# Two blocks of adaLN scale and shift in a two-layer trunk: raw weights as the stationary side of single-column matmuls

## The chip, the cores and the metric

The kernel runs on one core of one Trainium2 chip. The metric is the device time of one execution in microseconds; lower is better. All inputs, weights and results are float32 in device memory, and the kernel is one launch.

## The reference, cut to what matters

Two layers, each with a token mixer and a SwiGLU feed-forward part, over 512 tokens of 1024 features. Ahead of each part the tokens are normalized and modulated by scale and shift, which come from a conditioning vector `c` through a 1024 x 3072 matrix:

```
def ada_modulation(c, w, b):
    m = jax.nn.silu(c) @ w + b
    shift, scale, gate = jnp.split(m, 3, axis=-1)
...
    shift, scale, gate = ada_modulation(c, mix_ada_w[i], mix_ada_b[i])
    h = rms_norm(x, mix_pre_g[i]) * (1.0 + scale) + shift
    y = stick_breaking_mixer(h, sb_w_qkv[j], sb_w_o[j])
```

The change touches only the very first modulation (`mix_ada_w[0]`), and of it only the scale and shift of features 0 to 255. The rest of the work (attention with stick-breaking weights, three more modulations, the gated mixer, two feed-forward parts) is the same in both kernels.

## The kernel before, in words

Features lie in 8 blocks of 128. At the start the kernel loads the four token tiles of `x` (128 x 1024 each), normalizes them (`norm0`), transposes them with TensorE into feature-major tiles `xhT` (`turn0`; tile `tp` in the profile), applies scale and shift to one feature block at a time (`h0`, line 702, on ScalarE), and splits the result into a rounded high part `hTh` and a remainder `hTl`. Every product of the model is then three matmuls: high by high, high by low, low by high. The weights are split in the same way into `wh` (ScalarE, line 161) and `wl` (VectorE, line 162).

With block 0 of `h` the kernel starts the value projection (tiles `v`, weights "wv") and the query and key projection of the first pair of heads (`pq` and `pk`, weights "wqk"). It accumulates over the 8 feature blocks in order, so each block's scale and shift, for which the raw modulation matrix must be multiplied by `silu(c)` (the column tile `sc`), stands ahead of its matmuls.

The sums of `silu(c)` by the raw matrix are made in two ways. Blocks 0 and 1 are loaded as two raw tiles each (`ada`, 128 x 4 x 256: four input blocks, 128 columns of scale and 128 of shift), and go through `row0` and `scales`: TensorE multiplies a single column of `sc` as weights by 256 moving columns and sums over the 8 input blocks into one row in PSUM; VectorE copies the row; two matmuls with one partition turn it into two columns; VectorE adds the bias and multiplies. Blocks 2 to 7 are loaded two at a time as four raw tiles (128 x 2 x 512) and summed over input blocks on VectorE, eight instructions for each pair of blocks (`ada0_sum`, tile `acc`); four matmuls with a moving column of ones (`sums0`) then sum over the partitions and give columns.

```
    def sums0(ps, acc, k):
        for i in range(4):
            mm(ps[:, i : i + 1], acc[:, i * P : (i + 1) * P], onec, False, i == 3)
```

A scheduler lays out each engine's instructions from the order of the code and its own costs; in the part of the program that the change touches nothing else holds them in the order in which they are written. On the chip each engine runs its own list strictly in that order and waits on semaphores. Loads are issued from SyncE's queue, also in order; two buffers hold raw weights ("raw"), so a load of the next weights waits until the split of those two before is done.

In the profile one f32 matmul is two records of PE (and two weight loads of PEld); a transpose or a matmul of split operands is one.

Of the kernel before, what the change touches and what calls it, by code (L numbers as in the profile page):

```python
# [8 lines left out]
F32 = mybir.dt.float32  # L9
# [4 lines left out]
P = 128  # L14
# [3 lines left out]
KD = D // P  # L18
# [13 lines left out]
def trunk(ctx: ExitStack, tc: tile.TileContext, A: dict, out: bass.AP):  # L32
# [17 lines left out]
    def nm(s):  # L50
        uid[0] += 1
        return f"{s}_{uid[0]}"
# [4 lines left out]
    def bank(name, tag="b"):  # L57
        return psum.tile([P, 512], F32, tag=tag, bufs=6 if tag == "b" else 2, name=nm(name))
# [19 lines left out]
    dve = Vector()  # L78

    def pe_op(b):  # L80

        if pe["chain"] and pe["prev"] is not None:
            order(b, pe["prev"])
        pe["prev"] = b

    def order(b, before):
        tc.add_manual_dep(
            b.ins, before.ins.name,
            mybir.DependencyInfo(mybir.DependencyClass.NoSync, mybir.DependencyReason.DATA),
            reason="order",  # L90
        )

    def mm(o, l, r, start, stop, after=None):
        b = nc.tensor.matmul(o, l, r, start=start, stop=stop, skip_group_check=True)  # L94
        pe_op(b)
        if after is not None:
            order(b, after)
# [29 lines left out]
    raws = []  # L127
# [107 lines left out]
    def wget(src, look=3):  # L235

        n = taken[0]
        taken[0] += 1
        while len(got) < min(n + 1 + look, len(stream)):
            wemit()  # L240
        assert stream[n][3] == src, (stream[n][3], src)
        return got[n]
# [44 lines left out]
    stp = st0.__enter__()  # L287

    def ada0_raw(b, q):

        nk, n = (4, 256) if b < 2 else (2, 512)
        raw = stp.tile([P, nk, n], F32, tag="ra", bufs=8, name=nm("ada0"))
        load(raw[:], A["ada0s"][b, q] if b < 2 else A["ada0p"][b - 2, q])
        return raw
# [3 lines left out]
    x0, a0 = [], []  # L298
# [12 lines left out]
    a1 = [ada0_raw(1, q) for q in range(2)]  # L311
# [5 lines left out]
    oneb = consts.tile([P, 2], F32, name="oneb")  # L317
# [3 lines left out]
    sc = consts.tile([P, KD], F32, name="sc")  # L321
# [271 lines left out]
    def norm0(tt):  # L593
        xt = x0[tt]
        junk = npool.tile([P, D], F32, tag="n", name=nm("junk"))
        sx = small.tile([P, 1], F32, tag="sx", name=nm("sx"))
        act.activation(junk[:], xt, AF.Square, accum_out=sx[:])
        sd, r1 = rms(sx[:])
        dve.reciprocal(r1[:], sd[:])
        dve.tensor_scalar(xt, xt, r1[:, 0:1], None, ALU.mult)  # L600

    def turn0(tt):
        xt = x0[tt]
        for q in range(2):
            ps = bank("tp0")
            for k in range(4):
                kk = q * 4 + k
                transpose(ps[:, k * P : (k + 1) * P], xt[:, kk * P : (kk + 1) * P])
            for k2 in range(2):
                dst = xhT[q * 2 + k2][:, :, tt * P : (tt + 1) * P]  # L610
                src = ps[:, k2 * 256 : (k2 + 1) * 256].rearrange("p (a b) -> p a b", a=2)
                if q and tt < 2:
                    dve.tensor_copy(dst, src)
                else:
                    act.activation(dst, src, AF.Copy)
# [47 lines left out]
    def cols0(k):  # L663

        ps = bank("ab0", "p")
        mm(ps[:, 0:4], ident, add[:, k : k + 2, :].rearrange("p n a -> p (n a)"), True, False)
        return ps
# [8 lines left out]
        )  # L676
        return ab

    def row0(raws):

        ps = bank("ab0", "p")
        for q, raw in enumerate(raws):
            for k in range(4):
                mm(ps[0:1, :256], sc[:, q * 4 + k : q * 4 + k + 1], raw[:, k, :], q + k == 0, q * 4 + k == 7)
        row = stp.tile([P, 256], F32, tag="row", bufs=2, name=nm("row"))
        dve.tensor_copy(row[0:1, :], ps[0:1, :256])
        ps = bank("ab0", "p")
        for i in range(2):
            mm(ps[:, i : i + 1], row[0:1, i * P : (i + 1) * P], oneb[0:1, 0:1], True, True)
        return ps  # L690

    def scales(ps, k):

        ab = small.tile([P, 2, 2], F32, tag="ab", name=nm("ab"))
        dve.tensor_tensor(ab[:, 0, :], ps[:, :2], add[:, k, :], ALU.add)
        dve.tensor_tensor(ab[:, 0, :], ab[:, 0, :], mul[:, k, :], ALU.mult)
        return ab

    def h0(ab, i, k):

        xk = xhT[k // 2][:, k % 2, :]
        act.activation(xk, xk, AF.Identity, scale=ab[:, i, 0:1], bias=ab[:, i, 1:2])
        h, l = hTk(hT, k, 0, T)
        split(h, l, xk)
# [9 lines left out]
    norm0(1)  # L714
    turn0(0)
    norm0(2)
    ab0 = row0(a0)
    turn0(1)
    norm0(3)
    turn0(2)  # L720
# [1 line left out]
    wv0.append(wget(("wv", 0, 0), 0))  # L722
    a2 = [ada0_raw(2, q) for q in range(4)]
    h0(scales(ab0, 0), 0, 0)
    ab1 = row0(a1)
    wqk0.append(wget(("wqk", 0, 0), 0))
    vb = [bank("v0") for _ in range(NT)]
    pq0, pk0 = bank("pq"), bank("pk")
# [5 lines left out]
    for b in range(1, 4):  # L734

        ps = cols0(2 * b)
# [818 lines left out]
```

## Time and profile before

| | |
|---|---|
| time, median of 3 runs | 1135.93 us (1134.57 to 1136.39) |
| the profiled execution's own time | 1133.95 us |
| its span, first to last instruction | 1132.2 us |
| PE busy | 1110.9 us, 98% of the span |
| PEld, DVE, ACT busy | 999.9, 933.0, 596.6 us |
| granted TensorE clock, mean | 0.998 |

Engines are PE (matmuls), PEld (weight loads, beside PE), DVE (VectorE), ACT (ScalarE), POOL and SP (load queue). "L94" is a line of the kernel, here the helper that records every matmul, so that matmuls are told apart by their tiles: "ab<-ada,sc" writes tile `ab` from `ada` and `sc`. A row's idle time names what the engine waited for. The profiled execution was 1.98 us under the median of the timed runs.

### The profile page before, as it was taken

The page shows a single profiled execution, that of the slowest core. Times are in us where ns is not written, and L with a number is a line of the kernel's source. Part 1 is how long each engine was busy: PE and PEld are TensorE (multiplying, and loading weights), DVE is VectorE, ACT ScalarE, POOL GpSimd, SP SyncE. Part 2 cuts the span into 40 slices and gives each one's busy share as a digit, 9 for nine tenths or more (in the row PEclk, how much of TensorE's full clock was granted, in tenths as well). Part 3 has the DMA queues.
Part 4 walks back from the last instruction along what each step waited for, and adds up shares of the span by engine and source line. Part 5 has one row for each costly group of instructions (what it writes and reads, how often), then busy time and mean ns, then how long its engine had stood idle before and what let it go on. Part 6 is the DMA issues. An engine that isn't in the chain of part 4 may idle for free.

```text
span 1132.2 us, 18659 instructions
## 1 busy us (share of the span) xinstructions
PE 1110.9 (98%) x7436; PEld 999.9 (88%) x7436; DVE 933.0 (82%) x1223; ACT 596.6 (53%) x985; POOL 29.5 (3%) x53
## 2 busy tenths in 40 slices
PE   6999999999999999999999999999999999999997
PEld 4787878788999999998888988988999999999996
DVE  4988999958989898778686865759979898789996
ACT  6445655656655555572153624537455555465752
POOL 0120100000000000010000100001000000000000
PEclk9999999999999999999999999999999999999999
DMA  8876434214344343348886483324243434223242
GB/s 322 336 238 213 147 98 134 93 59 158 122 150 131 128 151 117 129 136 310 269 275 218 150 280 110 131 94 160 83 132 115 164 130 146 70 85 99 90 154 106
DMA packets 51356, 176.39 MB, mean 156 GB/s; under 512 B 6074, under 2 KB 9146, under 8 KB 51268
## 3 DMA queue, kind: packets, MB, share of 16 engines
q1 hardware_dynamic: 48708, 166.81, 43.6%
q0 software_dynamic: 2560, 8.39, 2.0%
q8 instruction: 58, 0.95, 0.3%
q14 instruction: 30, 0.25, 0.1%
HBM read 164.69 MB, written 8.39 MB: 153 GB/s over the span
## 4 chain that ended last, share of the span: by engine, by line
PE 88%; DVE 5%; ACT 3%; DMA 2%; issue 1%; SPq 0%; DVEq 0%; ACTq 0%
PE r L94 32%; PE y L94 16%; PE v L94 8%; PE pqk L94 7%; PE X L94 4%; PE gu L94 4%; PE Y L94 3%; PE u L94 3%; PE av L94 2%; PE z L94 2%; PE tw L102 1%; PE Z L94 1%; PE W L94 1%; PE tp L102 1%; PE ab L94 1%
## 5 line engine op out<-in xcount | busy, mean ns | idle before, releaser
L94 PE MATMUL r<-Sh,wl 128*128 128x256 f32 x608 | 170.0, 280 | 0.0
L94 PE MATMUL r<-Sh,wh 128*128 128x256 f32 x608 | 169.9, 279 | 0.0
L94 PE MATMUL r<-Sl,wh 128*128 128x256 f32 x608 | 169.8, 279 | 0.0
L161 ACT ACTIVATE wh<-raw 128x1024 fp32r<-128x1024 f32 x87 | 91.6, 1059 | 113.3 <-PE y L94 57.5
L94 PE MATMUL y<-wh,as 128*128 128x512 f32 x480 | 150.7, 391 | 0.0
L117 ACT ACTIVATE wh<-f 128x1024 fp32r<-128x1024 f32 x87 | 92.3, 1061 | 91.3 <-PE r L94 66.4
L70 DVE TENSOR_TENSOR wl<-f,wh 128x1024 fp32r<-128x1024 f32 x87 | 106.4, 1222 | 38.9 <-ACT wh L117 38.8
L162 DVE TENSOR_TENSOR wl<-raw,wh 128x1024 fp32r<-128x1024 f32 x87 | 105.8, 1221 | 38.2 <-ACT wh L161 37.5
L94 PEld LDWEIGHTS r<-Sl,wh 128*128 128x128 f32 x608 | 114.2, 188 | 0.0
L94 PEld LDWEIGHTS r<-Sh,wl 128*128 128x128 f32 x608 | 114.2, 188 | 0.0
L94 PEld LDWEIGHTS r<-Sh,wh 128*128 128x128 f32 x608 | 114.1, 188 | 0.0
L94 PEld LDWEIGHTS y<-wh,as 128*128 128x128 f32 x480 | 90.1, 188 | 18.6
L94 PE MATMUL y<-wl,as 128*128 128x512 f32 x240 | 93.8, 391 | 0.0
L94 PE MATMUL r<-hTh,wh 128*128 128x256 f32 x304 | 88.9, 293 | 0.6 <-DVE gu L70 0.6
L94 PE MATMUL r<-hTl,wh 128*128 128x256 f32 x304 | 84.8, 279 | 0.0
L94 PE MATMUL r<-hTh,wl 128*128 128x256 f32 x304 | 80.0, 279 | 0.0
L94 PEld LDWEIGHTS r<-hTh,wh 128*128 128x128 f32 x304 | 57.0, 188 | 5.9 <-DVE gu L70 2.4
L94 PE MATMUL r<-hTh,b 128*128 128x256 f32 x304 | 59.8, 279 | 0.0
L117 ACT ACTIVATE wh<-rawx 128x1024 fp32r<-128x1024 f32 x38 | 40.3, 1061 | 33.4 <-PE r L94 30.8
L94 PEld LDWEIGHTS r<-hTl,wh 128*128 128x128 f32 x304 | 57.2, 188 | 0.1
L94 PEld LDWEIGHTS r<-hTh,wl 128*128 128x128 f32 x304 | 55.0, 188 | 0.0
L94 PE MATMUL gu<-hTh,wh 128*128 128x256 f32 x192 | 54.0, 281 | 0.0
(272 smaller groups left out, 2960.7 us busy)
## 6 DMA issues: line engine op xcount, KB each, us to landing
rawada<-in_ada SPq DMA_DIRECT2D x80, 512.0 KB, 4.9
rawy<-in_wy SPq DMA_DIRECT2D x38, 512.0 KB, 3.5
rawx<-in_wx SPq DMA_DIRECT2D x38, 512.0 KB, 4.1
raw<-in_wdown SPq DMA_DIRECT2D x22, 512.0 KB, 4.6
raw<-in_wdn SPq DMA_DIRECT2D x22, 512.0 KB, 3.5
raw<-in_wqk SPq DMA_DIRECT2D x16, 512.0 KB, 4.5
ada<-in_ada0p SPq DMA_DIRECT2D x12, 512.0 KB, 9.0
raw<-in_wgu SPq DMA_DIRECT2D x12, 512.0 KB, 3.5
```

What stands on the lines that cost most here:

```text
L70: b = getattr(nc.vector, op)(*args, **kw)
L94: b = nc.tensor.matmul(o, l, r, start=start, stop=stop, skip_group_check=True)
L102: last_tp[0] = nc.tensor.transpose(o, i, ident)
L117: act.activation(hi, src, AF.Copy)
L161: act.activation(h[:], raw[:], AF.Copy)
L162: last_low[0] = nc.vector.tensor_tensor(l[:], raw[:], h[:].bitcast(F32), ALU.subtract)
```

## The change

The row is gone. `raw0` makes the two columns directly: for each of the 8 input blocks and for scale and shift, the raw 128 x 128 tile is the weights and the column of `sc` is what moves. That is 16 f32 matmuls for a feature block, all accumulated in one PSUM bank, in place of 8 matmuls with 256 moving columns, one copy on VectorE and two single-partition matmuls. `scales` and everything behind it are as they were, and no load is added, removed or moved in its queue.

```diff
-    def row0(raws):
+    def raw0(raws):
         ps = bank("ab0", "p")
         for q, raw in enumerate(raws):
             for k in range(4):
-                mm(ps[0:1, :256], sc[:, q * 4 + k : q * 4 + k + 1], raw[:, k, :], q + k == 0, q * 4 + k == 7)
-        row = stp.tile([P, 256], F32, tag="row", bufs=2, name=nm("row"))
-        dve.tensor_copy(row[0:1, :], ps[0:1, :256])
-        ps = bank("ab0", "p")
-        for i in range(2):
-            mm(ps[:, i : i + 1], row[0:1, i * P : (i + 1) * P], oneb[0:1, 0:1], True, True)
+                kk = q * 4 + k
+                for i in range(2):
+                    mm(
+                        ps[:, i : i + 1], raw[:, k, i * P : (i + 1) * P], sc[:, kk : kk + 1],
+                        kk + i == 0, kk + i == KD,
+                    )
         return ps
...
-    ab0 = row0(a0)
+    ab0 = raw0(a0)
...
-    ab1 = row0(a1)
+    ab1 = raw0(a1)
```

The scheduler also lays the first instructions of three engines out differently. Behind this stage the lists of all engines are the same in both kernels but for a few matmuls and casts that change places with a neighbour.

On PE, from the second transposed token tile on, before (`ab_45` is block 0's bank, `ab_47` its columns, `ab_65` block 1's bank; `x_2`, `x_3` and `x_4` are token tiles):

```order
L102 MATMUL tp_49_207<-identt,x_2_95 128x128 x4
L94 MATMUL ab_45_186<-ada_5_101,sc 1x256 x4
L94 MATMUL ab_45_186<-ada_6_103,sc 1x256 x4
L102 MATMUL tp_54_222<-identt,x_3_97 128x128 x4
L102 MATMUL tp_55_229<-identt,x_3_97 128x128
L94 MATMUL ab_47_197<-oneb,row_195 128x1 x2
L102 MATMUL tp_55_229<-identt,x_3_97 128x128 x3
L102 MATMUL tp_56_236<-identt,x_4_99 128x128 x4
L102 MATMUL tp_57_243<-identt,x_4_99 128x128 x4
L94 MATMUL ab_65_268<-ada_8_107,sc 1x256 x4
L94 MATMUL ab_65_268<-ada_9_109,sc 1x256 x4
L94 MATMUL v_70_286<-wh_250,hTh_132 128x512
```

and in the changed kernel, at the same place (block 0's bank is `ab_45`, block 1's is `ab_63`; `ab_78` is the bank of blocks 2 and 3):

```order
L102 MATMUL tp_47_210<-identt,x_2_95 128x128 x4
L94 MATMUL ab_45_186<-sc,ada_5_101 128x1 x8
L102 MATMUL tp_52_225<-identt,x_3_97 128x128 x4
L102 MATMUL tp_53_232<-identt,x_3_97 128x128 x4
L94 MATMUL ab_45_186<-sc,ada_6_103 128x1 x8
L102 MATMUL tp_54_239<-identt,x_4_99 128x128 x4
L102 MATMUL tp_55_246<-identt,x_4_99 128x128 x4
L94 MATMUL ab_63_271<-sc,ada_8_107 128x1 x8
L94 MATMUL ab_78_334<-add,identt 128x4
L94 MATMUL v_66_292<-wh_253,hTh_132 128x512
L94 MATMUL ab_63_271<-sc,ada_9_109 128x1 x8
L94 MATMUL v_66_292<-wl_254,hTh_132 128x512
```

The second half of block 1's sums moved behind the first value matmul, which needs block 0's `hTh`.

On ACT, from the first weight cast to the second, before (`wh_250` is the first "wv" tile, `wh_282` the first "wqk" tile, `ab_262` holds block 0's columns; the scale of block 1 is the next row):

```order
L161 ACTIVATE wh_250<-raw_105 128x1024
L615 ACTIVATE xhT_128<-tp_54_222 128x2x128
L615 ACTIVATE xhT_129<-tp_54_222 128x2x128
L615 ACTIVATE xhT_130<-tp_55_229 128x2x128
L615 ACTIVATE xhT_131<-tp_55_229 128x2x128
L615 ACTIVATE xhT_128<-tp_56_236 128x2x128
L615 ACTIVATE xhT_129<-tp_56_236 128x2x128
L615 ACTIVATE xhT_130<-tp_57_243 128x2x128
L615 ACTIVATE xhT_131<-tp_57_243 128x2x128
L702 ACTIVATE xhT_128<-xhT_128,ab_262 128x512
L117 ACTIVATE hTh_132<-xhT_128 128x512
L161 ACTIVATE wh_282<-raw_111 128x1024
```

and in the changed kernel, from the last token tile's evacuation on (`wh_253` and `wh_288` are the same two weights, `ab_265` and `ab_310` the columns of blocks 0 and 1):

```order
L615 ACTIVATE xhT_128<-tp_54_239 128x2x128
L615 ACTIVATE xhT_129<-tp_54_239 128x2x128
L615 ACTIVATE xhT_130<-tp_55_246 128x2x128
L615 ACTIVATE xhT_131<-tp_55_246 128x2x128
L161 ACTIVATE wh_253<-raw_105 128x1024
L702 ACTIVATE xhT_128<-xhT_128,ab_265 128x512
L117 ACTIVATE hTh_132<-xhT_128 128x512
L702 ACTIVATE xhT_128<-xhT_128,ab_310 128x512
L161 ACTIVATE wh_288<-raw_111 128x1024
L117 ACTIVATE hTh_132<-xhT_128 128x512
```

Both casts of weights moved: the first from ahead of all eight evacuations to behind them, the second from ahead of block 1's scale to behind it.

On DVE, from block 0's `hTl` to the end of the first eight sums of `ada0_sum`, before:

```order
L70 TENSOR_TENSOR hTl_133<-xhT_128,hTh_132 128x512
L162 TENSOR_TENSOR wl_283<-raw_111,wh_282 128x1024
L70 COPY row_277<-ab_65_268 1x256
L70 SCALAR_TENSOR_TENSOR acc_318<-ada_60_254,sc,acc_318 128x512
L70 TENSOR_TENSOR ab_304<-ab_67_279,add 128x2
L70 SCALAR_TENSOR_TENSOR acc_318<-ada_60_254,sc,acc_318 128x512
L70 TENSOR_TENSOR ab_304<-ab_304,mul 128x2
L70 SCALAR_TENSOR_TENSOR acc_318<-ada_61_256,sc,acc_318 128x512 x2
L70 TENSOR_TENSOR hTl_133<-xhT_128,hTh_132 128x512
L70 SCALAR_TENSOR_TENSOR acc_318<-ada_62_258,sc,acc_318 128x512 x2
L70 SCALAR_TENSOR_TENSOR acc_318<-ada_63_260,sc,acc_318 128x512 x2
```

and in the changed kernel:

```order
L70 TENSOR_TENSOR hTl_133<-xhT_128,hTh_132 128x512
L70 TENSOR_TENSOR ab_310<-ab_63_271,add 128x2
L70 TENSOR_TENSOR ab_310<-ab_310,mul 128x2
L162 TENSOR_TENSOR wl_289<-raw_111,wh_288 128x1024
L70 TENSOR_TENSOR hTl_133<-xhT_128,hTh_132 128x512
L70 SCALAR_TENSOR_TENSOR acc_324<-ada_58_257,sc,acc_324 128x512 x2
L70 SCALAR_TENSOR_TENSOR acc_324<-ada_59_259,sc,acc_324 128x512 x2
L70 SCALAR_TENSOR_TENSOR acc_324<-ada_60_261,sc,acc_324 128x512 x2
L70 SCALAR_TENSOR_TENSOR acc_324<-ada_61_263,sc,acc_324 128x512 x2
```

Four of the eight sums stood ahead of block 1's `hTl`; now all eight stand behind it, and block 1's columns and the split of the "wqk" weights stand ahead of them.

## The prediction

> **What bounds the kernel now.** First the page: busy times and the chain of work that ended last.
>
> ```profile
> PE 1110.9 (98%) x7436; PEld 999.9 (88%) x7436; DVE 933.0 (82%) x1223; ACT 596.6 (53%) x985; POOL 29.5 (3%) x53
> PE 88%; DVE 5%; ACT 3%; DMA 2%; issue 1%; SPq 0%; DVEq 0%; ACTq 0%
> ```
>
> TensorE is the bound of the whole. What the start is worth is read from the busy time in windows:
>
> ```profile
> 35.00:40.00 5.00, 4.83 (x21) 4.02 (x22) 4.86 (x8) 1.70 (x3) 0.00 (x0) 1.00 1.00 393
> 40.00:45.00 5.00, 4.62 (x26) 3.60 (x24) 4.83 (x8) 2.16 (x4) 0.00 (x0) 1.00 1.03 417
> 45.00:50.00 5.00, 5.00 (x22) 4.16 (x23) 4.86 (x9) 1.35 (x2) 0.00 (x0) 1.00 1.03 416
> 50.00:60.00 10.00, 10.00 (x49) 8.38 (x49) 9.86 (x11) 4.51 (x8) 3.43 (x8) 1.00 0.61 203
> ```
>
> PE is full from 45 us on, so a microsecond by which the matmuls there come later is a microsecond at the end. VectorE is full too from 35 to 60 us (4.86, 4.83, 4.86, 9.86): it has no room to give a delay back. The stage itself is in the chain of waits, in order of time (start, length, what):
>
> ```profile
> 10.29 1.97 PE tp L102 x8
> 12.26 4.46 PE ab L94 x16
> 16.71 0.70 PE tp L102 x5
> 17.41 0.53 PE ab L94 x4
> 17.94 1.35 PE tp L102 x11
> 19.30 3.54 PE ab L94 x16
> 24.88 0.55 PE ab L94 x4
> 35.17 3.02 PE v L94 x12
> 38.19 0.68 PE pq L94 x3
> ```
>
> The two rows of sums (4.46 and 3.54) and the turns into columns (0.53, 0.55) lie on the chain: 9.08 us of PE. The timeline shows who stands beside them (start, length, engine):
>
> ```profile
> 13.85 0.13 PEld L94 LDWEIGHTS ab<-ada,sc 128*1 128x1 f32 x1 [0.30 <-issue]
> 14.09 1.06 ACT L161 ACTIVATE wh<-raw 128x1024 fp32r<-128x1024 f32 x1
> 14.18 2.03 PEld L94 LDWEIGHTS ab<-ada,sc 128*1 128x1 f32 x10 [0.20 <-issue]
> 18.46 1.77 ACT L615 ACTIVATE xhT<-tp 128x256 f32<-128x256 f32 x6 [0.46 <-PE tp L102]
> 20.05 0.85 ACT L702 ACTIVATE xhT<-xhT,ab 128x512 f32<-128x512 f32 x1
> 20.94 0.63 ACT L117 ACTIVATE hTh<-xhT 128x512 fp32r<-128x512 f32 x1
> 21.48 1.04 ACT L161 ACTIVATE wh<-raw 128x1024 fp32r<-128x1024 f32 x1
> 22.55 1.23 DVE L162 TENSOR_TENSOR wl<-raw,wh 128x1024 fp32r<-128x1024 f32 x1 [0.25 <-ACT wh L161]
> 24.02 0.73 DVE L70 SCALAR_TENSOR_TENSOR acc<-ada,sc,acc 128x512 f32<-128x512 f32 x1
> 25.45 0.16 DVE L70 TENSOR_TENSOR ab<-ab,add 128x2 f32<-128x2 f32 x1 [0.70 <-PE ab L94]
> 26.19 0.15 DVE L70 TENSOR_TENSOR ab<-ab,mul 128x2 f32<-128x2 f32 x1
> 27.89 0.69 DVE L70 TENSOR_TENSOR hTl<-xhT,hTh 128x512 fp32r<-128x512 f32 x1
> 28.50 3.11 DVE L70 SCALAR_TENSOR_TENSOR acc<-ada,sc,acc 128x512 f32<-128x512 f32 x4
> 31.89 0.95 PE L94 MATMUL ab<-oneb,acc 128*128 128x1 f32 x8
> 32.80 0.50 PE L94 MATMUL pk<-hTh,wl 128*128 128x512 f32 x1
> ```
>
> Two readings matter. VectorE's eight sums `acc` begin at 24.02, four of them ahead of block 1's `hTl` (27.89), and end at 28.50 + 3.11 = 31.61; TensorE reaches the matmuls that need them at 31.89. They meet within 0.3 us: whatever delays `acc` from here delays PE. And the first sums of a row run in a slower gear: their weight loads are 0.42 apart until 13.85, then ten in 2.03, which is why the same 16 records took 4.46 us the first time and 3.54 the second.
>
> **The change, part by part.** *New matmuls.* The case has their like: the single-column matmuls behind `acc`, 128 x 128 f32 weights and one moving column. Eight records from 31.89 to the next start at 32.80 are 0.91/8 = 0.114 us each. A block's 16 matmuls are 32 records, 3.65 us; both blocks 7.30, against 9.08 now: PE works 1.78 us less.
>
> *Up to block 0's `hTh`.* PE now does 32 of these records and 16 transposes (1.35/11 = 0.123 each) from 12.26: 3.65 + 1.97, to 17.9. The slow gear lasts until 14.1; bounds for the price of a record in it are 0.114 and twice that, which puts the end between 17.9 and 18.8. I take 18.1, against 19.30: 1.2 us earlier. ACT's last evacuation ends 18.46 + 1.77 = 20.23 now, 0.93 behind the last transpose, so at 19.0. But the 1.06 us cast of the first weights, which now fills an idle stretch at 14.09, stands behind the evacuations: 20.1. Then 0.85 + 0.63: `hTh` at 21.6, where it is now (20.94 + 0.63 = 21.57). The gain is gone; VectorE's row copies cost nothing that ends late.
>
> *Up to block 1's `hTh`.* The second half of block 1's sums, 16 records, 1.82 us, is queued on PE behind the first value matmul (3.02/12 = 0.25 with its wait, 0.68/3 = 0.227 in a stream), which waits for that `hTh`. So 21.7 + 0.23 + 1.82 = 23.75, VectorE's two small steps (0.16, 0.15) and semaphores: columns at 24.1. ACT scales (0.85) to 24.95, then must cast the "wqk" weights (1.04, to 26.0), then `hTh` at 26.65.
>
> *VectorE.* Its list is strict: split of "wqk" after 26.0 (1.23), to 27.3; block 1's `hTl` (0.69), to 28.0; only then eight sums. One is 3.11/4 = 0.78: 6.2, to 34.2, against 31.61. The raw tiles do not matter: `acc` runs from 24.02 today, so they are there.
>
> *PE then.* Behind 23.75 it has 11 + 12 value records and six of `pq`, 6.6 us, and 0.25 for bias columns: done at 30.6. It waits 3.6 us for `acc`, with `pk` and the next block's matmuls queued behind. The columns' matmuls start at 34.2 instead of 31.89: 2.3 us late. In the next block the sums start behind two weight splits, as now, from a VectorE that is 2.6 us late:
>
> ```profile
> 36.75 4.68 DVE L70 SCALAR_TENSOR_TENSOR acc<-ada,sc,acc 128x512 f32<-128x512 f32 x6
> 41.65 0.95 PE L94 MATMUL ab<-oneb,acc 128*128 128x1 f32 x8
> ```
>
> They end at 41.43 now and PE is there at 41.65, another meeting within 0.3; late by 2.6 and 2.3, they meet again. I carry 2.6 us to the end, between 1.9 (the gear's best case, and waits somewhat shorter) and 3.2 (the slow record price).
>
> *The clock.* A wait of 3.6 us is new. What such a wait does stands at the end of the trace, in the windows after the last matmul:
>
> ```profile
> 1124.60:1126.80 2.20, 0.21 (x1) 0.00 (x0) 1.16 (x2) 1.02 (x3) 0.00 (x0) 1.00 0.68 238
> 1126.80:1132.00 5.20, 0.00 (x0) 0.00 (x0) 1.71 (x4) 0.00 (x0) 0.00 (x0) 0.50 0.29 101
> ```
>
> About 2 us after PE's last matmul the granted clock is 0.50. At the start it took from 10.29 to 14.18, 3.9 us of work, to get from 0.42 to 0.22 a step (the clock column shows 1.00 there, the steps show the gear). If the clock falls in the new wait, some 3.9 us run at half speed: up to 1.9 us of work lost, less where PE waits anyway (the value matmuls at 35.17 follow a wait for `hTh`). I take 1.5, between 0 and 2.2.
>
> Sum: 2.6 + 1.5 = 4.1 us on the profiled execution's 1133.95, 1138.05. That execution was 1.98 us under the median of 1135.93; added, **1140.0 us**.
>
> **The rivals.** *No fall of the clock*: PE's wait is too short for it, or broken into pieces. Then 2.6 remains: 1138.5. For it: today's waits of a microsecond or so leave the gear alone.
>
> *Slow gear until the value matmuls*: single-column matmuls may not count as work for the clock. Against it, nothing in this trace shows them at the start; for it, the gear rose only during the row sums, not during 1.97 us of transposes. Then 16 transposes cost 0.12 more each (1.97/8 = 0.25 against 0.123), 2.0, and the 48 records on the path to block 1's columns 0 to 0.114 more each: 2.0 to 7.5 in all. By the middle, less the 0.2 that the 18.1 holds already, 4.5 on top of the forecast's 1140.0: 1144.5 (1142 to 1147.5).
> [...]
>
> *The other side: PE's shorter work decides.* 1.78 us less, on a chain that is nearly all PE: 1135.93 - 1.8 = 1134.1. It needs `acc` at 31.61 or sooner, so block 1's `hTl` done by 25.4 instead of 28.0: that is where it tips. The strict lists of ACT and VectorE, with the two casts moved, speak against it; it happens if the sums are not really behind `hTl`, or the casts are hidden.
>
> *Swallowed*: a later wait that depends on a fixed time takes the 2.6 us back; 1135.9. PE full from 45 us on speaks against it.
>
> **How the numbers follow.** Chances: forecast 0.47 (1140.0), no fall of the clock 0.18 (1138.5), slow gear 0.25 (1144.5), PE's shorter work 0.05, swallowed 0.05. About 0.2%, 2.3 us, is what a measurement here can tell from no change: from 1133.7 to 1138.2 is the same. Of the no-fall case 0.13 lies above that, 0.05 within. So slower 0.47 + 0.25 + 0.13 = 0.85; same 0.05 + 0.05 = 0.10, the swallowed case and the rest of no-fall; faster 0.05, the shorter work, counted whole though 1134.1 is just at the bound. The range, 1137.0 to 1145.5, takes the no-fall case down to 1.1 us and the slow gear to somewhat over its middle; the two unlikely cases and a third of the slow gear, under 0.2, are left out.
>
> **What would show it.** Right: about 64 records `ab<-sc,ada` at 0.11 to 0.12 us each once the gear is up; block 0's `hTh` near 21.6; the first `acc` only near 28 and the last one ending near 34; a PE wait of some 3.6 us for `acc` ahead of `ab<-oneb,acc`; matmul steps twice as long for a few microseconds behind it; PE full from about 48 us on. Wrong in size: steps of 0.42 at the first value matmuls (slow gear), or none behind the wait (no fall). Wrong in kind: `acc` ended before 32, or PE not waiting for it.

## The result: slower by 0.7%, and the profile after

| | before | after |
|---|---|---|
| time, median of the runs | 1135.91 us (1133.98 to 1136.85, 6 runs) | 1145.32 us (1140.75 to 1147.62, 6 runs) |
| ratio of the times, 95% interval | | 1.0073 (1.0052 to 1.0094) |
| the profiled execution's own time | 1133.95 us | 1145.34 us |
| its span | 1132.2 us | 1143.5 us |
| first rise of the granted clock in the trace | 14.07 us | 35.93 us |

The ratio is 8.3 us (5.9 to 10.7); the two medians lie 9.4 us apart. Two lines of the page after, busy time and the chain that ended last:

```profile
PE 1119.5 (98%) x7460; PEld 1013.3 (89%) x7460; DVE 933.2 (82%) x1221; ACT 596.9 (52%) x985; POOL 29.5 (3%) x53
PE 80%; DVE 8%; DMA 7%; ACT 3%; issue 2%; SPq 0%; DVEq 0%; ACTq 0%
```

PE is busy for 8.6 us more (1119.5 against 1110.9), though at the prices of the prediction it had 1.8 us less to do. The chain of waits of the changed kernel says where (start, length, what):

```profile
10.69 1.97 PE tp L102 x8
12.66 3.20 PE ab L94 x16
15.87 1.81 PE tp L102 x8
17.68 3.21 PE ab L94 x16
20.88 1.81 PE tp L102 x8
22.69 3.63 PE ab L94 x18
26.32 0.63 PE v L94
26.95 3.22 PE ab L94 x16
...
30.59 0.81 ACT xhT L702
31.40 0.96 ACT wh L161
...
33.52 0.69 DVE hTl L70
34.21 0.67 DVE acc L70
...
53.80 3.01 PE v L94 x12
```

Sixteen single-column records take 3.20 to 3.22 us on the chain, 0.200 each, and eight transposes 1.81, 0.226 each: both at the price of a slow clock from the first to the last. Behind them stand ACT's scale, the "wqk" cast, block 1's `hTl` and then the sums. The last row is the start of the twelve value matmuls of feature block 4; in the kernel before that group stands here:

```profile
44.93 3.02 PE v L94 x12
```

That is 8.87 us later in the changed kernel. I use this group as the marker in all runs below but e9, whose order differs there. The timeline of the changed kernel shows the change of gear and the meeting of `acc` with PE:

```profile
25.06 0.63 ACT L117 ACTIVATE hTh<-xhT 128x512 fp32r<-128x512 f32 x1
33.58 0.63 PE L94 MATMUL v<-wh,hTh 128*128 128x512 f32 x1
34.01 0.63 PE L94 MATMUL v<-wl,hTh 128*128 128x512 f32 x1
34.12 6.26 DVE L70 SCALAR_TENSOR_TENSOR acc<-ada,sc,acc 128x512 f32<-128x512 f32 x8
36.05 0.39 PE L94 MATMUL v<-wh,hTh 128*128 128x512 f32 x1
36.28 0.39 PE L94 MATMUL v<-wl,hTh 128*128 128x512 f32 x1
40.44 1.05 PE L94 MATMUL ab<-oneb,acc 128*128 128x1 f32 x8 [0.60 <-DVE acc L70]
```

The value matmuls are 0.43 apart at 33.58 and 0.23 apart at 36.05, so the gear rose between the two. All eight sums ran in one block from 34.12 to 40.38, where they ended at 31.61 before; PE waited only 0.60 us for them. The windows behind:

```profile
35.00:40.00 5.00, 4.84 (x21) 3.73 (x19) 4.79 (x7) 1.07 (x1) 0.00 (x0) 1.00 0.95 370
40.00:45.00 5.00, 3.85 (x21) 3.32 (x22) 4.95 (x8) 2.56 (x4) 1.43 (x2) 1.00 0.84 305
45.00:50.00 5.00, 5.00 (x24) 4.14 (x23) 4.82 (x7) 1.06 (x1) 0.00 (x0) 1.00 0.99 358
50.00:60.00 10.00, 9.37 (x51) 7.68 (x49) 9.50 (x14) 3.52 (x5) 0.00 (x0) 1.00 1.03 415
```

From here the lists of the two kernels agree and the 8.9 us are carried on: the same ScalarE instructions stand 8.8 to 9.2 us later at 80, 240 and 480 us. At about 600 us, in the down projection of layer 0, the changed kernel's profile loses 2 us more. The waits from 575 to 615 us, first before, then after:

```profile
DVE A L70 <- DMA rawada<-in_ada: 1.2, 3, 0.8
```
```profile
DVE A L70 <- DMA rawada<-in_ada: 4.5, 2, 2.7
```

This is a wait for a load that the change does not touch. Between 480 and 620 us the profiles of other kernels shown below moved by -0.6 to 2.6 us against the same profile of before; e8, level with it to 0.2 us at 240 us, stood 1.6 later at 620. I take it for a difference between executions, of which the profiled one of before (1133.95, 1.96 under its median) was among the short ones; that was not tested on its own.

### The profile page after: what moved, and what is told of

Its sections match the earlier page's. It is cut to its first block, busy times and chain, and to the rows that moved or that the text cites. A ratio compares the mean times of both kernels' runs of the same rounds, so it can differ in the third digit from the quotient of the medians.

```text
span 1143.5 us, 18702 instructions
## 1 busy us (share of the span) xinstructions
PE 1119.5 (98%) x7460; PEld 1013.3 (89%) x7460; DVE 933.2 (82%) x1221; ACT 596.9 (52%) x985; POOL 29.5 (3%) x53
## 4 chain that ended last, share of the span: by engine, by line
PE 80%; DVE 8%; DMA 7%; ACT 3%; issue 2%; SPq 0%; DVEq 0%; ACTq 0%
PE r L94 31%; PE y L94 8%; PE v L94 7%; PE pqk L94 7%; DMA rawada<-in_ada 4%; PE X L94 4%; PE gu L94 4%; PE Y L94 3%; PE u L94 3%; PE av L94 2%; PE z L94 2%; PE tw L102 1%; PE Z L94 1%; PE W L94 1%; PE ab L94 1%
## 5 line engine op out<-in xcount | busy, mean ns | idle before, releaser
L94 PE MATMUL r<-Sh,wl 128*128 128x256 f32 x608 | 169.7, 279 | 0.0
L94 PE MATMUL r<-Sh,wh 128*128 128x256 f32 x608 | 169.6, 279 | 0.0
L94 PE MATMUL r<-Sl,wh 128*128 128x256 f32 x608 | 169.6, 279 | 0.0
L94 PE MATMUL y<-wh,as 128*128 128x512 f32 x480 | 150.9, 391 | 1.2 <-DVE G L70 1.2
L70 DVE TENSOR_TENSOR wl<-f,wh 128x1024 fp32r<-128x1024 f32 x87 | 106.4, 1223 | 38.9 <-ACT wh L117 35.7
L94 PEld LDWEIGHTS r<-Sl,wh 128*128 128x128 f32 x608 | 114.1, 188 | 0.0
L94 PEld LDWEIGHTS r<-Sh,wl 128*128 128x128 f32 x608 | 114.1, 188 | 0.0
L94 PEld LDWEIGHTS r<-Sh,wh 128*128 128x128 f32 x608 | 114.0, 187 | 0.0
L94 PEld LDWEIGHTS y<-wh,as 128*128 128x128 f32 x480 | 90.1, 188 | 20.2 <-DVE G L70 1.6
L94 PE MATMUL y<-wl,as 128*128 128x512 f32 x240 | 93.7, 390 | 0.0
L94 PE MATMUL r<-hTh,wh 128*128 128x256 f32 x304 | 88.7, 292 | 0.5 <-DVE gu L70 0.4
L94 PE MATMUL r<-hTl,wh 128*128 128x256 f32 x304 | 84.7, 279 | 0.0
L94 PE MATMUL r<-hTh,wl 128*128 128x256 f32 x304 | 79.9, 279 | 0.0
L94 PEld LDWEIGHTS r<-hTh,wh 128*128 128x128 f32 x304 | 56.9, 187 | 5.8 <-DVE gu L70 2.2
L94 PE MATMUL r<-hTh,b 128*128 128x256 f32 x304 | 59.8, 279 | 0.0
L94 PEld LDWEIGHTS r<-hTl,wh 128*128 128x128 f32 x304 | 57.1, 188 | 0.1
L94 PEld LDWEIGHTS r<-hTh,wl 128*128 128x128 f32 x304 | 55.0, 188 | 0.0
L94 PE MATMUL gu<-hTh,wh 128*128 128x256 f32 x192 | 54.0, 281 | 0.0
```

Of the source, the lines that this page charges most:

```text
L70: b = getattr(nc.vector, op)(*args, **kw)
```

## The experiments

Three things had changed together: the form of the matmuls, the order of the lists, and, as the profile shows, the clock. The theory after the result: single-column matmuls leave the clock low, and this costs some 6 us; the order costs the rest. The rivals: the order costs nearly all; or the single-column matmuls are slow in themselves, whatever the clock.

The marker is the start of block 4's value matmuls in the profiled execution against 44.93; the ratio is of the timed runs, with its 95% interval, against runs of the kernel before that were made beside each kernel's own (their medians are 1135.5 to 1136.5 us). "Half" tells when the trace has the granted clock at one half again after its first rise.

| kernel | moving columns | order | median us | ratio | clock up first | half again | marker |
|---|---|---|---|---|---|---|---|
| changed kernel | 1 | its own | 1145.3 | 1.0073 (1.0052 to 1.0094) | 35.93 | no | +8.87 |
| e1 | 128 | the changed kernel's | 1140.8 | 1.0045 (1.0028 to 1.0061) | 13.81 | 34.29 to 41.11 | +4.83 |
| e2 | 1 | e3's | 1141.2 | 1.0056 (1.0036 to 1.0077) | 23.12 | 26.54 to 29.95 | +4.25 |
| e3 | 128 | scheduler's | 1134.8 | 0.9997 (0.9986 to 1.0008) | 13.56 | no | -1.33 |
| e4 | 1, early work | scheduler's, close to the changed kernel's | 1143.6 | 1.0077 (1.0062 to 1.0092) | 7.26 | 14.09 to 34.57 | +7.49 |
| e5 | 128 | e3's, sums late | 1139.7 | 1.0026 (1.0011 to 1.0041) | 13.96 | no | +0.80 |
| e6 | 128 | e1's, sums early | 1135.3 | 0.9994 (0.9982 to 1.0007) | 16.61 | no | +1.19 |
| e7 | rows, then 1 | scheduler's | 1139.7 | 1.0035 (1.0023 to 1.0046) | 14.01 | 24.25 to 31.07 | +3.62 |
| e8 | 128, early work | scheduler's | 1135.9 | 0.9993 (0.9981 to 1.0005) | 4.35 | 11.18 to 14.59 | -0.33 |
| e9 | 128, more early work | scheduler's | 1136.6 | 1.0006 (0.9991 to 1.0021) | 6.69 | 34.00 to 37.41 | other order |
| e10 | 128, wait filled | the changed kernel's | 1138.1 | 1.0013 (1.0001 to 1.0025) | 11.32 | no | +1.43 |
| e11, e12 | e5 again | | 1139.9, 1139.1 | one run each | 14.26, 15.51 | 34.74 to 41.56, 32.58 to 39.40 | +3.80, +3.50 |

**Form and order, two by two.** In e1 and e3 the same matmuls, with the same weights, move 128 equal columns instead of one, of which one is used:

```diff
-                        ps[:, i : i + 1], raw[:, k, i * P : (i + 1) * P], sc[:, kk : kk + 1],
+                        ps[:, i * P : (i + 1) * P], raw[:, k, i * P : (i + 1) * P], sc[:, kk : kk + 1].to_broadcast([P, P]),
...
-        return ps
+        return ps[:, 0 : 2 * P : P]
```

With that edit alone the scheduler lays the lists out in another order (e3; three of the eight `acc` stand ahead of block 1's `hTl`, five behind, and all single sums of block 1 ahead of the first value matmul). In e1 and e2 an order is written out by hand, a list of instructions per engine (in e2 without the load queue): for e1 that of the changed kernel, for e2 (one column) that of e3.

```diff
+    for pins in (PIN_PE, PIN_Activation, PIN_DVE, PIN_SP):
+        there = [made[f"I-{n}"] for n in pins]
+        for b, a in zip(there[1:], there):
+            order(b, a)
```

> The changed kernel with its own order of instructions on every engine pinned, but the column of silu(c) is read 128 times (a moving operand of 128 equal columns, 128 output columns, of which one is used). A record costs the same weight load. Theory A (single-column matmuls do not count as work for TensorE's clock, which is why the slow gear lasted to 35.9 us): the steps halve near 14 to 16 us, as in the kernel before; what is left is the order, 2.6 us, so about 1138.5 us, up to 1140 if the wait for the sums lets the clock fall. Theory B (the order of the casts and sums costs it all, the gear only follows from waits): unchanged, 1145.

> The changed kernel's single-column matmuls, with the order on every engine pinned to the one that the scheduler makes for the 128-column form: first weight cast ahead of the evacuations, all of block 1's sums ahead of the first value matmul, four of the eight accumulations ahead of block 1's low part. Theory A: the slow gear still lasts until the value matmuls have run some 3 to 6 us, the sums' matmuls start near 38 instead of 31.9: 1141 to 1143.5 us. Theory B: at or below the kernel before, 1134 to 1136.

> 128 moving columns and the order that the scheduler makes for them, which is nearly that of the kernel before. Both causes are gone under either theory: TensorE's work is 1.8 us shorter than with the rows, the meeting with the eight accumulations at 31.6 stays. Theory A and B: 1134 to 1136 us, the kernel before or up to 1.8 us under it; a result over 1138 would speak for a third cause, such as the weight loads themselves.

Of e1, the row where PE waits for `acc`, from the timeline, and two windows around it (the third number from the right of a window is the granted clock; the helper lines L94, L102 and L70 are L113, L121 and L89 here, and L112, L120 and L88 in e2, where lines were added above them):

```profile
34.08 1.72 PE L113 MATMUL ab<-oneb,acc 128*128 128x1 f32 x8 [3.41 <-DVE acc L89]
```
```profile
30.87:34.29 3.42, 0.21 (x2) 0.21 (x2) 3.28 (x6) 1.06 (x1) 0.00 (x0) 1.00 1.02 411
34.29:37.70 3.41, 3.41 (x13) 3.02 (x13) 2.74 (x4) 1.67 (x3) 1.42 (x2) 0.50 0.74 233
```

In the changed kernel's own order, with a clock that rose at 13.81, the prediction's wait is there, 3.41 us, and the clock falls behind it: the eight records took 1.72 against 0.95 before. Order with a fall of the clock costs 5.1 us by the ratio (3.2 to 6.9), less than the changed kernel's 8.3, and the marker stands at +4.83 against +8.87. In e3 the wait for `acc` is down to 0.68 us, no fall is seen, and the loss is gone.

Of e2, which has single columns in e3's order, the chain of waits and the windows:

```profile
12.89 6.62 PE ab L112 x32
19.51 3.52 PE tp L120 x16
23.03 3.57 PE ab L112 x32
26.60 4.45 PE v L112 x12
```
```profile
19.71:23.12 3.41, 3.41 (x19) 3.41 (x17) 1.30 (x2) 2.03 (x7) 0.00 (x0) 1.00 0.85 294
23.12:26.54 3.42, 3.42 (x32) 3.42 (x32) 1.17 (x2) 2.88 (x5) 0.00 (x0) 1.00 0.25 97
26.54:29.95 3.41, 3.41 (x9) 2.64 (x9) 3.33 (x7) 1.80 (x3) 0.00 (x0) 0.50 0.44 131
29.95:33.36 3.41, 3.41 (x17) 2.85 (x16) 3.29 (x5) 1.67 (x2) 0.00 (x0) 1.00 1.00 386
```

This profile decides the disputed price. The first 32 records took 6.62 us, 0.207 each; the second 32, right after a stretch of transposes, 3.57, 0.112 each; the value matmuls behind those went at half clock again. The trace has the clock up at 23.12 and down at 26.54. So the record's price goes with the clock; behind 3.32 us of transposes and 0.09 of single-column records it was up, at 23.12, behind 3.42 us of nothing but single-column records, PE never idle, it was at one half, and behind 3.41 us nearly all of value matmuls it was up again, at 29.95. In e3's order single columns cost 1.0056 against 0.9997, some 6.7 us. The rival in which the records are slow in themselves falls with the 0.112. Nor does the form change a record's price: from start to start it is 0.213 us at half clock and 0.112 at full clock, with one moving column (half clock in the changed kernel, full clock in e2) and with 128 (e6). What differed with the form was the clock.

Transposes alone were followed by a rise elsewhere too: in e10 the clock rose at 11.32, and up to then PE had run nothing but transposes: 2.06 us in nine records from 5 to 10 us, and from 9.91 on the second eight. The weight loads go with the clock as their records do: those of the single-column records start 0.213 us apart at half clock (the changed kernel, 16 in 3.54 us) and 0.112 at full clock (e2).

**Part of the change, and earlier work.** e7 keeps the rows for block 0 and uses single columns for block 1 alone (`ab0 = row0(a0)`). e4 is the changed kernel with four f32 matmuls of 512 columns on a constant tile ahead of `norm0(0)`; e8 adds the same to e3:

```diff
+    zt = stp.tile([P, 512], F32, name="zt")
+    nc.gpsimd.memset(zt[:], 1.0)
+    zb = bank("zb", "p")
+    for i in range(4):
+        mm(zb[:], zt[:, :P], zt[:], i == 0, i == 3)
```

> Half of the change: block 0 by rows as before, block 1 by single columns; order as the scheduler makes it (block 1's matmuls all ahead of the first value matmul, but the eight accumulations all behind block 1's low part). The rows raise the clock near 14 us as before; 32 single-column records behind the last transposes, 3.6 us, are long enough to let it fall once: 1138 to 1141. If single columns counted as work: 1136 to 1138.5 from the order alone.

> The changed kernel with four extra f32 matmuls of 512 columns on a constant tile at the very start, in the 7 us in which TensorE has nothing to do; order as the scheduler makes it, close to the changed kernel's. Theory A: the clock is up before the first transposes; if single columns then count as nothing, it falls again within 4 to 7 us of them and the time is 1141 to 1144; if the clock holds through them, only the order is left, 1138 to 1139. Theory B: 1145.

> A try at beating both kernels: 128 equal moving columns, the good order, and four wide matmuls on a constant tile in the first 7 us. The clock is up before the first transposes, which saves about 1.0 us of transposes and 0.9 of the first sums against e3 (1134.8), as far as loads and the eight accumulations let it through: 1133 to 1134.5 us.

Windows of e7, over its single-column records and the one behind:

```profile
20.83:24.24 3.41, 2.83 (x24) 2.66 (x24) 0.32 (x2) 0.91 (x2) 0.00 (x0) 1.00 0.66 270
24.24:27.66 3.42, 2.57 (x6) 2.11 (x7) 2.33 (x3) 3.21 (x5) 0.00 (x0) 0.50 0.02 5
```

In e7, with the rows of block 0, the clock rose at 14.01 as before (14.07), and behind block 1's single columns, PE busy for 2.83 of 3.41 us, it was at one half again from 24.25. e7 costs 4.0 us (2.6 to 5.2); the scheduler also put all eight sums behind block 1's `hTl` in it, so this is the price of the single columns and of that order together. In e4 the clock was up at 7.26 and down at 14.09, while the first 16 single-column records ran, and stayed down to 34.57, through all the others: raising it early did not help a stage that did not hold it, 1.0077 against 1.0073. The 4 to 7 us that the expectation gave the fall were the author's estimate; it came 1.65 us after the first of these records, at 12.44 on the chain. PE had waited for `x` until 11.05 as well, so the fall itself does not show the columns' part as cleanly as e2 does. Two of the changed kernel's own six runs, 1143.48 and 1140.75, have a mean granted clock of 0.991, near e4's 0.989, where the other four have 0.997 or 0.998: an early rise that was lost again would give that, but no trace of those two was kept. In e8 it was lost while PE waited for `x` (1.09 us of work from 7.76 to 11.18), came back at 14.59 behind transposes and 128-column matmuls, and nothing was gained.

**The order by itself.** On VectorE, e6 is e1 with four of the eight sums moved ahead, and e5 is e3 with the three sums that stood ahead moved behind:

```diff
 # e6 against e1, DVE's list
 hTl (block 0)
+acc x2
 ab, ab (block 1's columns)
+acc x2
 wl (wqk)
 hTl (block 1)
-acc x8
+acc x4
```
```diff
 # e5 against e3, DVE's list
 wl (wqk)
 ab
-acc
 ab
-acc x2
 hTl (block 1)
-acc x5
+acc x8
```

> The 128-column form with the changed kernel's order on TensorE, ScalarE and the load queue (e1: 1140.8 us), but four of the eight accumulations ahead of block 1's low part on VectorE, as in the kernel before. Theory: the sums end near 31 instead of 34, TensorE's wait and with it the fall of the clock go: 1135 to 1137. If the casts on ScalarE or the place of block 1's matmuls cost it, 1139 to 1141.

> The 128-column form in the order of e3 (1134.8 us) on every engine, but for VectorE: all eight accumulations stand behind block 1's low part, and block 1's columns ahead of them, as in the changed kernel. If this place is what the order costs (theory: the eight sums meet TensorE with nothing to spare), the sums' matmuls start near 31.5 instead of 29.7 and the time is 1136.6 us, up to 1138.5 if the longer wait lets the clock fall. If the casts on ScalarE or the place of block 1's matmuls cost it, 1134.8 as e3.

Moving four sums (e6) took the whole of e1's loss away: 0.9994. Moving three the other way (e5) brought a loss, 1.0026, but its profiled execution, 1135.7, was the fastest of its ten and had no fall of the clock. Two more profiled executions of the same kernel:

> A second look at e5_wide_sums_late (median 1139.7, profiled execution 1135.7 without a fall of the clock). If its executions differ by whether the clock falls in PE's wait of 2.5 us for block 2's sums, a profiled execution of 1139 to 1141 shows half clock for some 3 us behind that wait; one near 1135.7 shows none.

> A third look at e5_wide_sums_late, for the same question: a profiled execution above 1138.5 with half clock behind the wait of 2.5 us, or one near 1135.7 without. A profiled execution above 1138.5 without half clock would mean that the difference lies elsewhere.

The row with PE's wait from e5's timeline, and from its chain the value matmuls of block 2 and the marker:

```profile
31.87 0.83 PE L113 MATMUL ab<-oneb,acc 128*128 128x1 f32 x6 [2.53 <-DVE acc L89]
```
```profile
35.70 3.06 PE v L113 x12
...
45.73 3.02 PE v L113 x12
```

and the same three of e11:

```profile
32.43 0.83 PE L113 MATMUL ab<-oneb,acc 128*128 128x1 f32 x6 [2.53 <-DVE acc L89]
```
```profile
36.28 5.46 PE v L113 x12
...
48.73 3.02 PE v L113 x12
```

The kernel and the wait are the same; in one execution the clock held, in the other it was half from 34.74 to 41.56 and twelve value matmuls took 5.46 instead of 3.06 us. From PE's restart behind the wait to the marker are 13.86 us in e5, 16.30 in e11 and 15.89 in e12: the fall costs 2.0 to 2.4 us where it happens. Two of the three profiled executions had it, and the mean granted clock of e5's ten timed runs points the same way: 0.998 in the one of 1135.7, 0.994 to 0.996 in the nine others.

Why the clock held in one of these executions and fell in the two others was not shown. PE's wait lies at 29.34 to 31.87 in e5, 29.90 to 32.43 in e11 and 29.99 to 32.54 in e12. In e5 the clock held with PE busy for 2.57 us from 31.03 to 34.44 and for 2.24 from there to 37.85; in e11 it fell at 34.74, behind 3.42 us of which PE was busy for 2.31; in e12 it fell at 32.58, 0.04 us behind the wait.

e10 is e1 with PE kept at work where it waits: seven f32 matmuls of 256 columns on a constant tile, into unused columns of the bank.

```diff
+        if b == 1:
+            zt = stp.tile([P, 256], F32, name="zt")
+            nc.gpsimd.memset(zt[:], 1.0)
+            for i in range(7):
+                mm(ps[:, 256:512], zt[:, :P], zt[:], False, False)
         ab = sums0(ps, acc, 2 * b)
```

> 128 equal moving columns in the changed kernel's order, as in e1_wide_same_order (1140.8), with seven f32 matmuls of 256 columns on a constant tile (14 records, some 3.1 us) put where PE waits for block 2's sums. Theory: e1's loss of 4.9 us is 2.6 of order (the sums end 2.6 us late) and the rest the clock that falls in that wait. Then the clock stays full and the time is 1138 to 1139.5, and 0 to 0.5 us later if the filling overruns the wait. Rival: the clock's fall costs nothing since PE waits in the next block anyway; then it is 1140.5 to 1141.5 as e1.

The filling and the sums' matmuls behind it, in e10's timeline:

```profile
29.40 3.18 PE L113 MATMUL ab<-zt 128*128 128x256 f32 x14
...
32.98 1.05 PE L113 MATMUL ab<-oneb,acc 128*128 128x1 f32 x8 [0.39 <-DVE acc L89]
```

The clock stayed up and the time went from 1.0045 to 1.0013: with the fall kept away, the order costs 1.5 us (0.1 to 2.8). e10's profiled start was also early (clock up at 11.32), so the marker alone (+1.43 against +4.83) would give the fall too much. From PE's restart behind the wait to the marker are 15.68 us in e1 and 13.38 in e10: by the profiles the fall costs 2.3 us of e1's 4.83, and the order 2.5.

**A version that beats both?** e9 is e3 with work on a constant tile in two places, six matmuls ahead of the first transposes and three behind the first token tile's, so that the clock is up and held.

```diff
+    busy(6)
     norm0(0)
...
     turn0(0)
+    busy(3, last_tp[0])
```

> 128 equal moving columns in the scheduler's own order, and 18 records of work on a constant tile in two places at the start: six f32 matmuls of 512 columns ahead of the first transposes, three behind the first token tile's. If the clock goes by PE's recent work and transposes keep it up once it is up, the gear stays full from about 5 us on, the first transposes and sums run at full pace and the time is 1133.0 to 1135.0, about a microsecond under the same kernel without it (1134.8). If the start is set by the loads of x and not by PE, it is 1134.5 to 1136, the same.

It did not: 1136.6, 1.0006. The start was held (clock up from 6.69 on), but the profile has half clock from 34.00 to 37.41, behind another wait of PE, 0.97 us for `hTh`. No version here is measurably faster than before; e3 and e6 are level with it. The ranges put down before the runs were missed by e1, e5, e8 and e9, each time to the slow side, by 0.6 to 1.4 us.

## Why the prediction was right, and where its steps failed

Forecast 1140.0, measured 1145.3: slower, as said, and inside the range by 0.2 us. That it is inside is luck: the six runs go from 1140.75 to 1147.62, and the forecast's own mechanism gives 5.3 us less. The mechanism that happened is that of the rival "slow gear until the value matmuls" (0.25, 1144.5), added to the order's cost, and the forecast's own second term did not happen.

- *Lists and what stands behind what: right.* The first cast stood behind the evacuations, the second half of block 1's sums behind the first value matmul, the eight sums behind block 1's `hTl`, and took 6.26 us where 6.2 was said.
- *End of the transposes and first sums, 18.1: failed.* It was 22.69, where block 1's records begin on the chain. The step took over from the trace of before that the gear rises at 14.1. That rise came during the row sums, which the change removes; in the changed kernel it came at 35.93. By 0.200 a record and 0.226 a transpose, the first 32 records and the 16 transposes between them took 10.03 us instead of 5.8. With it went `hTh` of block 0, 25.69 instead of 21.6, the first `acc`, 34.12 instead of 28, and the last one, 40.38 instead of 34.2.
- *PE's wait of 3.6 us and the fall of the clock, 1.5 us: failed here.* The wait was 0.60, since PE's own work in front of it took longer at half clock, and the clock, up at 35.93, did not fall. As a mechanism it exists: e1 shows the wait at 3.41 and the fall, e1 against e10 and e5 against e11 and e12 put the fall at 2.0 to 2.4, above the 1.5 I took and about at my bound of 2.2.
- *The order's 2.6 us: right in kind, and in size as far as the runs tell.* e10 gives 1.5 (0.1 to 2.8) by the timed runs and 2.5 by its profile beside e1's, e5 against e3 without a fall 2.1 (sums' matmuls at 31.87 and 29.74), the changed kernel against e2 1.9 by the difference of their ratios, whose intervals overlap.
- *The slow gear's 4.5: mis-sized.* e2 against e3 puts it at 6.7, the changed kernel less the order's 1.5 to 2.5 at 5.8 to 6.8. I took the middle of 2.0 to 7.5, because no row showed a record in the slow gear; it was 0.200 on the chain and 0.213 from start to start, near the upper price of 0.228. The rival's 1144.5 came close in part because it also held the 1.5 of a fall that did not come: 2.6 + 1.5 + 4.5 stood for about 1.9 + 0 + 6.5.
- *PE's shorter work: no gain was measured.* Even where order and clock are mended the ratio is 0.9997 (0.9986 to 1.0008, e3).

In the changed kernel the transposes come in groups of 1.81 us between single-column records of 3.20 to 3.21, and the clock did not rise among them; where 16 transposes stood together, in e2 (3.52 us from 19.51), it rose at 23.12.

## What to carry to other kernels

A record of a matmul with one moving column (an f32 matmul is two) took 0.112 us at full clock and 0.213 at half (e2, the changed kernel), and 32 of them in a row, PE busy for 3.42 of 3.42 us, were followed by half clock (e2). When a change replaces work at the start of a kernel, ask first whether the removed work was what raised the clock, and take none of the old timings behind it over until that is answered. And eight sums moved behind one wait in a strict queue cost 1.5 to 2.5 us here by themselves, and 2.0 to 2.4 more where the clock fell in or behind the wait that they make for PE.

## What was not expected of the hardware

PE busy all the time was not enough to keep the granted clock: 32 records of 128 x 128 weights with one moving column kept PE busy for 3.42 of 3.42 us (e2, 23.12 to 26.54) and the clock fell; behind the same records with 128 moving columns it rose at 16.61 in e6, where they were 3.35 of the 3.41 us before and transposes the rest. What in the form makes the difference was not shown. Behind the first rise the traces have half clock for 3.41 us (e2, e8, e9), 6.82 (e1, e7, e11, e12) or 20.48 (e4). The same kernel with the same wait of 2.53 to 2.55 us kept the clock in one execution and lost it in two others, 1135.7 against 1139.1 and 1139.9 us: one profile of a kernel with such a wait does not tell what its median will be.
